# Rows made from the mixer's scaled tiles, the mixer one tile up, and the down groups behind the joint part

## The chip, the cores and the metric

The kernel runs on one core of a Trainium2 chip. A core has TensorE (PE, the matmuls), VectorE (DVE), ScalarE (ACT) and GpSimd (POOL), and DMA queues, of which SyncE (SP) issues most. The metric is the time of one execution on the device in microseconds; lower is better. The time before is a median of three runs.

## The reference

The model has two layers over 1024 tokens of 1024 channels. Each layer is a token mixer and a SwiGLU FFN of 2816 columns, each behind an RMSNorm that is scaled and shifted by a conditioning vector. Layer 0 mixes by a causal convolution, layer 1 by trailing means:

```python
for i in range(DEPTH):
    sh_m, sc_m, g_m, sh_f, sc_f, g_f = split(silu(c) @ ada_w[i] + ada_b[i])
    h = modulate(rms_norm(x, norm_mix_g[i]), sh_m, sc_m)
    y = conformer_conv(h, ...) if i % 2 == 0 else multiscale_pool(h, ...)
    x = x + (1.0 + g_m) * y
    h = modulate(rms_norm(x, norm_ffn_g[i]), sh_f, sc_f)
    y = (silu(h @ w_gate) * (h @ w_up)) @ w_down
    x = x + (1.0 + g_f) * y
return rms_norm(x, final_g)
```

`multiscale_pool` takes, in four groups of channels, the mean of the last 2, 4, 8 or 16 tokens less the token, then a 256 by 256 matrix per group and a scale. All data is float32.

## The kernel before

Activations lie as 8 tiles (`KT`) of 128 channels by 512 tokens for each of two chunks of tokens, A (index 0) and B (index 1). A float32 product is made of three products of rounded halves: each tile is split into a high part (`hhi`, `ghi`, made by ACT) and a low part (`hlo`, `glo`, made by DVE or POOL as the tile less its high part), and weights likewise. So one 128-channel step costs three matmuls; the gate and up products of one ff-tile (128 of the 2816 columns) are 48 matmuls, and the down products of two ff-tiles for one chunk (`ffn_p2`) are 48 too.

The change lies in layer 1, around what is called the joint part. First, ff-tiles 0 to 7 of chunk A run plainly: the list `us` holds units in the order gate/up of f (`ffn_p1`), down products of the two tiles before (`ffn_p2`), gate/up of f + 1, and so on. While TensorE does that, chunk B's pool mixer runs on the other engines: its root (sum of squares, `var` and `rstd` as small matmuls, then the scaled tiles `t<-x,gains,ny`), its windows (`win`), the mixed tiles split into `mxhi` and `mxlo`, then on TensorE the `y` matmuls (48), whose results are added to `x` (`pool_out`). Then B's second norm is made (`norm`, giving `hhi` and `hlo` of B).

Then comes the joint part for ff-tiles 8 to 21 of both chunks. There the products of A and B with the two halves of the channels are formed by a scheme with fewer products, which takes combined operands: `joint_rows` makes the rows t1, t2, t3, t4 (each four tiles, split into high and low) from the tiles of A and B. It rebuilds each whole tile by adding high and low part. t1, t4 and the first half of B's normed tiles (`front`) are put into DRAM (`keep`) and streamed back later, since there is no room. `joint_unit` runs one unit: `block(..., "w11")`, `block(..., "w12")`, then the block on t2, on t1, on t3 and the rest, for gate, then for up. The first unit also runs the down products of A's tiles 6 and 7 behind its first blocks.

Behind the joint part stand the last two groups of its down products, which `alone` emits one after the other (48 + 48 matmuls); outputs go to the two spare PSUM banks there. Then `ffn_mixed` does ff-tiles 0 to 7 of chunk B: `before` holds gate/up of f = 0 and of f = 1, `pairs` the rest.

The order on TensorE is written by hand: `add`, `unit` and `need` append units to a list that is emitted in that order. The other engines' tasks are generators (`put`), of which the tile framework's priorities set the order: an urgent or eager task (`put_eager`) goes first, others have lower priority. `PSUM` has 8 banks, which `output(name, spread)` hands out. Tags of pools and their buffer counts say how many tiles of a kind there are (`"acc"`, `"win"`, `"ada"`, `"raw"`).

Of the kernel before, what the change touches and what calls it, by code (L numbers as in the profile page):

```python
# [16 lines left out]
P = 128  # L17
D = 1024
# [45 lines left out]
T2_AT, T3_AT = ((0, 1), (0, 1), (1, 0), (1, 0)), ((0, 1), (1, 0), (0, 1), (0, 1))  # L64
# [58 lines left out]
def trunk(ctx, tc, xT, c, vec, ada, adan, w1, w2, wgu, wdn, wpl, wph, out):  # L123
# [455 lines left out]
    def norm(ch, l, ffn, key, keep=False, squares=None, ks=range(KT), **kw):  # L579
# [7 lines left out]
        for k in ks:  # L587
# [398 lines left out]
    def ffn_p1(ch, l, f, pick, soon=False):  # L986
        def emit(take):
# [189 lines left out]
    class Downs:  # L1177
# [25 lines left out]
        def slot(self):  # L1203
# [198 lines left out]

    def joint_rows():

        ha, hb = st["h", 0], st["h", 1]
        half = KT // 2
        for name in ("t1", "t4", "front"):
            st["kept", name] = [[kept.tile([P, 512], F32, name=nm(name)) for _ in range(2)] for _ in range(half)]
        st["t1"], st["t2"], st["t3"] = [], [], []

# [9 lines left out]
        def whole(h, t):  # L1420
            V_.tensor_tensor(t, f32(h[0]), f32(h[1]), op=ADD)
            return t
        for k in range(half):
            keep("front", k, hb[k])
            a, c, d = whole(ha[k], window(512, "ha")), whole(hb[k], window(512, "hb")), whole(hb[k + half], window(512, "hb"))
            yield
            V_.tensor_tensor(a, a, c, op=SUB)
            V_.tensor_tensor(c, d, c, op=SUB)
            V_.scalar_tensor_tensor(d, a, -1.0, d, op0=MUL, op1=SUB)
            st["t2"].append(split(d, [wslot(B, n, F32R, at * ALIGN, 512) for n, at in zip(("t2hi", "t2lo"), T2_AT[k])]))  # L1430
            yield
            b = whole(ha[k + half], temp(512))
            V_.scalar_tensor_tensor(b, d, -1.0, b, op0=MUL, op1=SUB)
# [3 lines left out]
            st["t3"].append(split(c, [wslot(A, n, F32R, at * ALIGN, 512) for n, at in zip(("t3hi", "t3lo"), T3_AT[k])]))  # L1437
# [554 lines left out]
```

## Time and profile before

| | |
|---|---|
| median of 3 runs | 1816.73 us (1815.53 to 1817.51) |
| profiled execution | 1817.02 us |
| its span in the profile | 1815.2 us |
| granted TensorE clock, mean | 0.989 |
| PE busy | 1765.0 us (97%) |
| DVE busy | 1315.9 us (72%) |
| ACT busy | 940.4 us (52%) |
| POOL busy | 513.9 us (28%) |

Busy times are sums over the span; they can overlap. In the rows of the timeline a time stands first, then the length, engine, line, operation, the written tile and what it is made from, and in brackets the idle time of the engine just ahead with the instruction that ended it. L117 and L140 are the lines of helpers that record every vector instruction and every matmul, so rows are told apart by the names of tiles. A row of matmuls xN that starts at one time covers N matmuls in a row.

### The profile page before, as it was taken

The page shows a single profiled execution, that of the slowest core. Times are in us where ns is not written, and L with a number is a line of the kernel's source. Part 1 is how long each engine was busy: PE and PEld are TensorE (multiplying, and loading weights), DVE is VectorE, ACT ScalarE, POOL GpSimd, SP SyncE. Part 2 cuts the span into 40 slices and gives each one's busy share as a digit, 9 for nine tenths or more (in the row PEclk, how much of TensorE's full clock was granted, in tenths as well). Part 3 has the DMA queues.
Part 4 walks back from the last instruction along what each step waited for, and adds up shares of the span by engine and source line. Part 5 has one row for each costly group of instructions (what it writes and reads, how often), then busy time and mean ns, then how long its engine had stood idle before and what let it go on. Part 6 is the DMA issues. An engine that isn't in the chain of part 4 may idle for free. (4 is left out here: it accounts for less than half of the span.)

```text
span 1815.2 us, 24581 instructions
## 1 busy us (share of the span) xinstructions
PE 1765.0 (97%) x8930; PEld 1477.8 (81%) x8930; DVE 1315.9 (72%) x2107; ACT 940.4 (52%) x1439; POOL 513.9 (28%) x550
## 2 busy tenths in 40 slices
PE   9999999999999999999999999997999999998997
PEld 7777777888888887899998888875888888886997
DVE  7689847897764239899887867797666566648685
ACT  4776765777656366555555465444323233333553
POOL 0389723987823111201114414210000000000102
PEclk9999999999999999999999999998999999999999
DMA  9968775989979898877766568756655555584552
GB/s 301 284 179 260 176 165 161 246 206 234 229 196 226 216 226 193 233 201 207 210 171 150 139 155 199 171 151 218 208 186 197 186 197 186 197 268 103 141 150 59
DMA packets 133293, 353.13 MB, mean 195 GB/s; under 512 B 13490, under 2 KB 23858, under 8 KB 133171
## 3 DMA queue, kind: packets, MB, share of 16 engines
q1 hardware_dynamic: 105808, 265.56, 43.0%
q0 software_dynamic: 26208, 84.95, 26.3%
q8 instruction: 70, 1.15, 0.2%
q10 hardware_dynamic: 1154, 1.05, 0.2%
q14 instruction: 53, 0.43, 0.1%
HBM read 341.02 MB, written 10.49 MB: 194 GB/s over the span
## 5 line engine op out<-in xcount | busy, mean ns | idle before, releaser
L117 ACT CAST w<-raw 128x512 fp32r<-128x512 f32 (+1 forms) x338 | 276.5, 822 | 185.5 <-PE dn L140 55.8
L117 DVE SCALAR_TENSOR_TENSOR x<-dn,gains,x 128x512 f32<-128x512 f32 (+1 forms) x360 | 262.0, 735 | 118.3 <-PE dn L140 113.3
L140 PE MATMUL dn<-ghi,w 128*128 128x512 f32 (+1 forms) x992 | 316.6, 386 | 1.4 <-DMA w<-in_wdn_dram 0.8
L140 PE MATMUL gate<-hhi,w 128*128 128x512 f32 (+1 forms) x928 | 284.1, 374 | 0.6 <-ACT hhi L117 0.6
L140 PE MATMUL up<-hhi,w 128*128 128x512 f32 (+1 forms) x928 | 284.5, 374 | 0.0
L117 ACT ACTIVATE w<-raw 128x1024 fp32r<-128x1024 f32 (+1 forms) x182 | 175.5, 964 | 198.0 <-PE up L140 63.5
L117 POOL TENSOR_TENSOR pa<-pa,pr 128x512 f32<-128x512 f32 x176 | 252.8, 1584 | 18.3 <-ACT pr L117 15.5
L452 POOL DMA_DIRECT2D w<-in_wgu_dram x76 | 68.4, 904 | 650.9 <-ACT w L117 641.4
L140 PEld LDWEIGHTS dn<-ghi,w 128*128 128x128 f32 x992 | 185.3, 189 | 37.0 <-DMA w<-in_wdn_dram 1.2
L140 PEld LDWEIGHTS gate<-hhi,w 128*128 128x128 f32 x928 | 171.0, 188 | 32.9 <-ACT hhi L117 0.7
L140 PEld LDWEIGHTS up<-hhi,w 128*128 128x128 f32 x928 | 171.0, 188 | 31.0
L140 PE MATMUL dn<-glo,w 128*128 128x512 f32 (+1 forms) x496 | 191.2, 385 | 3.0 <-POOL glo L117 2.9
L140 PE MATMUL dn<-gpair,w 128*128 128x512 f32 x672 | 173.4, 396 | 8.8 <-DVE x L117 8.7
L140 PE MATMUL gate<-hlo,w 128*128 128x512 f32 (+1 forms) x464 | 173.5, 374 | 0.3 <-DVE hlo L117 0.3
L140 PE MATMUL up<-hlo,w 128*128 128x512 f32 (+1 forms) x464 | 173.3, 374 | 0.0
L117 DVE SCALAR_TENSOR_TENSOR ca<-u,vecs,ca 128x512 f32<-128x512 f32 x244 | 170.6, 747 | 1.0
L140 PEld LDWEIGHTS dn<-gpair,w 128*128 128x128 f32 x672 | 127.8, 191 | 38.8 <-DVE x L117 6.5
L117 DVE TENSOR_TENSOR w<-raw,w 128x512 fp32r<-128x512 f32 (+1 forms) x156 | 121.0, 781 | 35.4 <-ACT w L117 34.2
L117 ACT ACTIVATE pr<-u,vecs 128x512 f32<-128x512 f32 x176 | 120.2, 717 | 29.2 <-POOL pa L117 21.5
L117 DVE TENSOR_TENSOR t<-t,up 128x512 f32<-128x512 f32 (+1 forms) x79 | 51.4, 652 | 108.4 <-PE up L140 107.5
L1168 POOL DMA_DIRECT2D w<-in_wgu_dram x40 | 34.9, 879 | 266.5 <-ACT w L117 81.0
L140 PEld LDWEIGHTS dn<-glo,w 128*128 128x128 f32 x496 | 93.9, 189 | 19.5 <-POOL glo L117 3.9
(254 smaller groups left out, 3327.7 us busy)
## 6 DMA issues: line engine op xcount, KB each, us to landing
raw<-in_wgu_dram SPq DMA_DIRECT2D x148, 512.0 KB, 5.6
t<-t SPq DMA_DIRECT2D x224, 256.0 KB, 5.0
w<-in_wgu_dram POOLq DMA_DIRECT2D x76, 512.0 KB, 8.2
raw<-in_wdn_dram SPq DMA_DIRECT2D x74, 512.0 KB, 5.7
adaw<-in_ada_dram SPq DMA_DIRECT2D x64, 512.0 KB, 4.8
raw<-in_w_dram SPq DMA_DIRECT2D x42, 512.0 KB, 6.6
w<-in_wdn_dram POOLq DMA_DIRECT2D x34, 512.0 KB, 8.0
adaw<-in_adan_dram SPq DMA_DIRECT2D x32, 512.0 KB, 6.6
```

The lines of the kernel that those rows point to most:

```text
L117: self.last = self.order(getattr(self.eng, name)(out, *args, **kw))
L140: last_mm[0] = nc.tensor.matmul(out, lhsT, rhs, start=start, stop=stop, **kw).ins.name
L452: order(nc.gpsimd.dma_start(as_src(lo), src, accum_op=ADD))
L1168: order(nc.gpsimd.dma_start(lo, src, accum_op=ADD))
```

## The change

1. The root of B's pool mixer becomes a task of its own, `stats_whole`, which is urgent; `pool_whole` waits for its result and is eager.
2. `pool_out` and what follows come one unit earlier in `us` (at `len(us) - 5` instead of `len(us) - 4`), so the y matmuls stand ahead of gate/up of ff-tile 5 instead of behind it.
3. `wholes` makes the eight whole tiles of A while the mixer runs. `joint_rows` no longer starts from B's normed halves: it waits for the norm's `rstd` alone, makes each tile of B once as `scaled(k)`, combines from that, and splits only the second half of B's tiles there. `front` is one float32 tile for each k instead of a high and a low one, and is split into `hhi` and `hlo` in the last joint unit. The rows' places (`T2_AT`, `T3_AT`, `TURNED`) change, t4's tiles move from tag `"acc"` (2 buffers) to `"win"` (3). The g tiles of A's ff-tiles 6 and 7 move into `"ada"` tiles (`home`).
4. `alone(second, final)` fetches the final group's down weights with the first group and loads them when 4 outputs are left, and sends its outputs to all 8 banks in turn (`output(n, True)`). Gate/up of B's ff-tile 1 is put between the two groups of 48 down matmuls.

On TensorE, around the y matmuls; names are `up` (up products of an ff-tile), `dn` (down products), `y` (the mixer's products from `mxhi`, `mxlo`). Before:

```order
5329 L140 MATMUL up_10806<-hhi_9856,w_10730 128x512
5330 L140 MATMUL up_10806<-hlo_9857,w_10730 128x512
5331 L140 MATMUL up_10806<-hhi_9856,w_10731 128x512
5332 L140 MATMUL y_10882<-mxhi_10476,w_10801 128x512
5333 L140 MATMUL y_10882<-mxlo_10477,w_10801 128x512
5334 L140 MATMUL y_10882<-mxhi_10476,w_10802 128x512
```

And after:

```order
5281 L141 MATMUL dn_10805<-ghi_10657,w_10675 128x512
5282 L141 MATMUL dn_10805<-glo_10658,w_10675 128x512
5283 L141 MATMUL dn_10805<-ghi_10657,w_10676 128x512
5284 L141 MATMUL y_10827<-mxhi_10399,w_10739 128x512
5285 L141 MATMUL y_10827<-mxlo_10400,w_10739 128x512
5286 L141 MATMUL y_10827<-mxhi_10399,w_10740 128x512
```

Before, the y matmuls follow the up products of ff-tile 5; after, they follow the down products of ff-tiles 2 and 3, and stand 48 rows earlier.

On VectorE, in the middle of the combined rows (`ha`, `hb` are the rebuilt tiles of A and B, `t_` scaled tiles and temporaries, `whole` the tiles of A made ahead, `t1lo` to `t3lo` the low parts of the rows). Before:

```order
1387 L117 TENSOR_TENSOR ha_11491<-hhi_9846,hlo_9847 128x512
1388 L117 TENSOR_TENSOR hb_11493<-hhi_10987,hlo_10988 128x512
1389 L117 TENSOR_TENSOR t2lo_11467<-hb_11461,t2hi_11466 128x512
1390 L117 TENSOR_TENSOR t_2213_11484<-t_11470,t_2212_11483 128x512
1391 L117 TENSOR_TENSOR ha_11491<-ha_11491,hb_11493 128x512
1392 L117 TENSOR_TENSOR hb_11495<-hhi_10995,hlo_10996 128x512
1393 L117 TENSOR_TENSOR hb_11493<-hb_11495,hb_11493 128x512
1394 L117 TENSOR_TENSOR t1lo_11508<-ha_11491,t1hi_11507 128x512
```

And after:

```order
1339 L118 SCALAR_TENSOR_TENSOR t_11109<-whole_10633,t_11109 128x512
1340 L118 TENSOR_TENSOR t_11174<-t_11174,up_11058 128x512
1341 L118 TENSOR_TENSOR hlo_11218<-t_11169,hhi_11217 128x512
1342 L118 SCALAR_TENSOR_TENSOR whole_10653<-t_11109,whole_10653 128x512
1343 L118 SCALAR_TENSOR_TENSOR x_1_80<-dn_11201,gains,x_1_80 128x512
1344 L118 TENSOR_TENSOR t1lo_11289<-whole_10647,t1hi_11288 128x512
1345 L118 TENSOR_TENSOR t2lo_11134<-t_11109,t2hi_11133 128x512
1346 L118 SCALAR_TENSOR_TENSOR x_2_81<-dn_11209,gains,x_2_81 128x512
```

The rebuilding rows (`<-hhi,hlo`) are gone from here, and evictions to x now stand among the combinations.

On TensorE, behind the joint part, at the boundary between the two groups of down matmuls. Before:

```order
7004 L140 MATMUL dn_14946<-gpair_11867,w_14877 128x512 x3
7005 L140 MATMUL dn_14946<-gpair_11868,w_14877 128x512 x3
7006 L140 MATMUL dn_14959<-gpair_11865,w_14956 128x512 x3
7007 L140 MATMUL dn_14959<-gpair_11866,w_14956 128x512 x3
7008 L140 MATMUL dn_14970<-gpair_11867,w_14956 128x512 x3
```

And after:

```order
6972 L141 MATMUL dn_14919<-gpair_11835,w_14855 128x512 x3
6973 L141 MATMUL dn_14919<-gpair_11836,w_14855 128x512 x3
6974 L141 MATMUL gate_14937<-hhi_14586,w_14676 128x512
6975 L141 MATMUL gate_14937<-hlo_14587,w_14676 128x512
6976 L141 MATMUL gate_14937<-hhi_14586,w_14677 128x512
```

The second group no longer follows the first at once; the 48 gate/up matmuls of ff-tile 1 stand between.

The diff, cut to its core:

```diff
 GATE_SLOTS = (6, 9, 12, 14, 17, 19, 22, 24)
-T2_AT, T3_AT = ((0, 1), (0, 1), (1, 0), (1, 0)), ((0, 1), (1, 0), (0, 1), (0, 1))
+T2_AT, T3_AT = ((0, 1), (0, 1), (1, 0), (0, 1)), ((1, 0), (0, 1), (0, 1), (1, 0))
+TURNED = ((27,), (22, 25, 26, 29))
 UP_SLOTS = (3, 6, 9, 11, 14, 17, 20, 23)
...
-    def gated(ch, f, outs, soon=False, held=None):
+    def gated(ch, f, outs, soon=False, held=None, home=None):
 
-        hi, lo = st["g", ch.i, f] = gslots(ch)
+        if home is None:
+            hi, lo = st["g", ch.i, f] = gslots(ch)
+        else:
+            g = raws.tile([P, D], F32R, tag="ada", name=nm("gpair"), bufs=ADA_BUFS)
+            st.setdefault("G", []).append(g)
+            hi, lo = st["g", ch.i, f] = g[:, FRONT], g[:, BACK]
         t = temp(ch.n) if held is None else temp(ch.n, "ny", 2)
...
 
-    def alone(downs):
+    def alone(downs, later=None):
 
         def emit(take):
+            if later is not None:
+                later.fetch()
             while downs.todo:
-                downs.slot()
+                downs.slot(lambda n: output(n, True))
+                if later is not None and len(downs.todo) == 4:
+                    later.load(later.dps[0])
             reserve[0] = 0
...
 
+    def wholes():
+
+        st["whole"] = []
+        for h in st["h", 0]:
+            t = wslot(B, "whole", F32, 0, 512)
+            V_.tensor_tensor(t, f32(h[0]), f32(h[1]), op=ADD)
+            st["whole"].append(t)
+            yield
+
     def joint_rows():
 
-        ha, hb = st["h", 0], st["h", 1]
         half = KT // 2
-        for name in ("t1", "t4", "front"):
+        for name in ("t1", "t4"):
             st["kept", name] = [[kept.tile([P, 512], F32, name=nm(name)) for _ in range(2)] for _ in range(half)]
+        st["kept", "front"] = [kept.tile([P, 512], F32, name=nm("front")) for _ in range(half)]
         st["t1"], st["t2"], st["t3"] = [], [], []
+        hb = st["h", 1] = [None] * KT
+        while ("rstd", 1) not in st:
+            yield "wait"
+        rstd = st.pop(("rstd", 1))
 
...
 
-        def whole(h, t):
-            V_.tensor_tensor(t, f32(h[0]), f32(h[1]), op=ADD)
+        def scaled(k):
+            t = temp(512)
+            V_.scalar_tensor_tensor(t, x[1][k], scale_f[:, KT + k : KT + k + 1], rstd, op0=MUL, op1=MUL)
+            S_.activation(t, t, AF.Identity, bias=shift(1, 3, k))
             return t
         for k in range(half):
-            keep("front", k, hb[k])
-            a, c, d = whole(ha[k], window(512, "ha")), whole(hb[k], window(512, "hb")), whole(hb[k + half], window(512, "hb"))
+            c, d = scaled(k), scaled(k + half)
+            a, b = st["whole"][k], st["whole"][k + half]
+            sync.dma_start(st["kept", "front"][k], c)
             yield
+            hb[k + half] = split(d, (slot(B, "hhi"), slot(B, "hlo")))
             V_.tensor_tensor(a, a, c, op=SUB)
-            V_.tensor_tensor(c, d, c, op=SUB)
-            V_.scalar_tensor_tensor(d, a, -1.0, d, op0=MUL, op1=SUB)
-            st["t2"].append(split(d, [wslot(B, n, F32R, at * ALIGN, 512) for n, at in zip(("t2hi", "t2lo"), T2_AT[k])]))
+            e = window(512, "hb")
+            V_.tensor_tensor(e, d, c, op=SUB)
             yield
-            b = whole(ha[k + half], temp(512))
+            V_.scalar_tensor_tensor(d, a, -1.0, d, op0=MUL, op1=SUB)
+            st["t2"].append(split(d, [wslot(B if k else A, n, F32R, at * ALIGN, 512) for n, at in zip(("t2hi", "t2lo"), T2_AT[k])]))
             V_.scalar_tensor_tensor(b, d, -1.0, b, op0=MUL, op1=SUB)
+            yield
             st["t1"].append(split(a, [slot(B, n) for n in ("t1hi", "t1lo")]))
...
             yield
-            st["t3"].append(split(c, [wslot(A, n, F32R, at * ALIGN, 512) for n, at in zip(("t3hi", "t3lo"), T3_AT[k])]))
-            keep("t4", k, split(b, [tmp.tile([P, TMPW], F32R, tag="acc", name=nm("t4"), bufs=2) for _ in range(2)]))
+            st["t3"].append(split(e, [wslot(A if k < half - 1 else B, n, F32R, at * ALIGN, 512) for n, at in zip(("t3hi", "t3lo"), T3_AT[k])]))
+            keep("t4", k, split(b, [tmp.tile([P, PHALO + TMPW], F32R, tag="win", name=nm("t4"), bufs=3)[:, :512] for _ in range(2)]))
             yield
...
             V_.tensor_tensor(ra, ra, left, op=ADD)
+            if last:
+                front = []
+                for src in st["kept", "front"]:
+                    t = slot(A, "front", F32)
+                    sync.dma_start(t, src)
+                    hi, lo = slot(A, "hhi"), slot(A, "hlo")
+                    S_.copy(hi, t)
+                    V_.tensor_tensor(lo, t, f32(hi), op=SUB)
+                    front.append((hi, lo))
             if first:
...
             if last:
-                st["h", 1] = [tuple(t) for t in streamed("front", A)] + hb[half:]
+                st["h", 1] = front + hb[half:]
             else:
...
                 V_.scalar_tensor_tensor(qb, qb, -1.0, sg[2], op0=MUL, op1=MUL)
-                if "G" not in st:
-                    st["G"] = [raws.tile([P, D], F32R, tag="ada", name=nm("gpair"), bufs=ADA_BUFS) for _ in range(2)]
+                if len(st["G"]) == 2:
                     st["G"] += [raws.tile([P, D], F32R, tag="raw", name=nm("gpair")), wide("gpair", F32R)]
...
                                  i == 0, i + 1 == len(mates)))
-        return us, [alone(d) for d in (mine[-2][0], mine[-1][0])]
+        (second,), (final,) = mine[-2:]
+        return us, [alone(second, final), alone(final)]
 
...
 
-    def pool_whole(ch):
+    def stats_whole(ch):
         acc = yield from sum_sq(x[ch.i], ch.n)
-        st["spread", ch.i] = mean_rsqrt(acc, ch.n, True, "col2")
+        st["rstd", ch.i] = yield from mean_rsqrt(acc, ch.n, True, "col2")
+
+    def given(key):
+        return st.pop(key)
+        yield
+
+    def pool_whole(ch):
+        while ("rstd", ch.i) not in st:
+            yield "wait"
+        st["spread", ch.i] = given(("rstd", ch.i))
         yield from pool(ch)
+        T["wholes"] = Task(wholes(), False, 0)
+        T["wholes"].eager = True
+
+    def mixed_norm(squares):
+        st["rstd", 1] = yield from mean_rsqrt(squares.acc, 512, True)
 
...
     for f in range(0, WHOLE, 2):
-        us += [ffn_p1(A, 1, f, True), joint_pend, ffn_p1(A, 1, f + 1, True)]
+        home = True if f + 2 == WHOLE else None
+        us += [ffn_p1(A, 1, f, True, home=home), joint_pend, ffn_p1(A, 1, f + 1, True, home=home)]
         joint_pend = ffn_p2(A, 1, [f, f + 1], True)
...
         if i == 1:
-            put(("pool", 1), lambda: pool_whole(B), at=0, delay=DELAY_AMONG)
-        if i == len(us) - 4:
+            put(("stats", 1), lambda: stats_whole(B), True, delay=DELAY_AMONG)
+            put_eager(("pool", 1), lambda: pool_whole(B))
+        if i == len(us) - 5:
             need(("pool", 1))
...
                 pool_out(B, 1, q, squares)
-            put(("nf", 1), lambda: norm(B, 1, True, ("hn", 1), True, squares, [k + q for k in range(KT // 2) for q in (0, KT // 2)]),
-                True, delay=DELAY_AMONG)
+            put(("nf", 1), lambda: mixed_norm(squares), True, delay=DELAY_AMONG)
+            put_eager("rows", joint_rows)
     need(("nf", 1))
-    unit(lambda take: st.__setitem__(("h", 1), st["hn", 1]))
-    put_eager("rows", joint_rows)
     joint, last = ffn_joint(1, WHOLE)
     add(joint)
-    unit(lambda take: setattr(B, "made", B.made + KT // 2))
     before, pairs, rest = ffn_mixed(B, 1, 2, WHOLE, True, ("final_a", lambda: final(A)))
...
     put_eager(("T", 1), lambda: combined(B, (A, A, B, B)))
-    add(last)
-    add(before[1:])
+    add(last[:1] + before[1:] + last[1:])
     paired(B, pairs)
```

More of the change, by code (lines that the diff above doesn't have):

```diff
@@ L264, in gslots @@
         turned = ch.i == 0 and ch.made >= NF and (ch.made - NF) % 4 == 0
-        odd = (ch.made // (KT // 2) + ch.i + turned) % 2
+        odd = (ch.made // (KT // 2) + ch.i + turned + (ch.made in TURNED[ch.i])) % 2
         ch.made += 1
@@ L577, in modulated, with norm @@
             lows.append(V_.last.ins.name)
-    def norm(ch, l, ffn, key, keep=False, squares=None, ks=range(KT), **kw):
+    def norm(ch, l, ffn, key, keep=False, squares=None, **kw):
         h = [(slot(ch, "hhi"), slot(ch, "hlo")) for _ in range(KT)]
@@ L586, in norm @@
         lows = []
-        for k in ks:
+        for k in range(KT):
             modulated(ch, l, ffn, h, rstd, k, lows if kw else None)
@@ L983, in update, with ffn_p1 @@
         V_.scalar_tensor_tensor(xs, b, gate[:, l * KT + d : l * KT + d + 1], xs, op0=MUL, op1=ADD)
-    def ffn_p1(ch, l, f, pick, soon=False):
+    def ffn_p1(ch, l, f, pick, soon=False, home=None):
         def emit(take):
@@ L995, in emit @@
                         pace()
-            gated(ch, f, outs, soon)
+            gated(ch, f, outs, soon, home=home)
         return emit, (wgu[l, f, 0], wgu[l, f, 1])
-    def gated(ch, f, outs, soon=False, held=None):
-        hi, lo = st["g", ch.i, f] = gslots(ch)
+    def gated(ch, f, outs, soon=False, held=None, home=None):
[5 more added lines that the diff above has]
+            hi, lo = st["g", ch.i, f] = g[:, FRONT], g[:, BACK]
         t = temp(ch.n) if held is None else temp(ch.n, "ny", 2)
@@ L1201, in load, with slot @@
             self.tiles[dp] = wt
-        def slot(self):
+        def slot(self, out=None):
             d = self.todo.pop(0)
@@ L1896, in trunk @@
     pooled(rest[:-1], A, OUT_AT)
+    def stats_whole(ch):
+        acc = yield from sum_sq(x[ch.i], ch.n)
+        st["rstd", ch.i] = yield from mean_rsqrt(acc, ch.n, True, "col2")
+    def given(key):
+        return st.pop(key)
+        yield
     def pool_whole(ch):
-        acc = yield from sum_sq(x[ch.i], ch.n)
-        st["spread", ch.i] = mean_rsqrt(acc, ch.n, True, "col2")
+        while ("rstd", ch.i) not in st:
+            yield "wait"
+        st["spread", ch.i] = given(("rstd", ch.i))
         yield from pool(ch)
+        T["wholes"] = Task(wholes(), False, 0)
+        T["wholes"].eager = True
+    def mixed_norm(squares):
+        st["rstd", 1] = yield from mean_rsqrt(squares.acc, 512, True)
     us, joint_pend = [], rest[-1]
     for f in range(0, WHOLE, 2):
-        us += [ffn_p1(A, 1, f, True), joint_pend, ffn_p1(A, 1, f + 1, True)]
+        home = True if f + 2 == WHOLE else None
+        us += [ffn_p1(A, 1, f, True, home=home), joint_pend, ffn_p1(A, 1, f + 1, True, home=home)]
         joint_pend = ffn_p2(A, 1, [f, f + 1], True)
```

2 lines of the change are left out of this document (1 added, 1 removed).

## The prediction

> **What bounds the kernel now.** I read the stretches of 40 us first, then the waits of TensorE, then its rows and VectorE's in the two stretches where it is short. Columns of the first view: busy time and instructions of PE, PEld, DVE, ACT and POOL, the granted clock, the DMA share, GB/s.
>
> ```profile
> 1160.00:1200.00 40.00, 40.00 (x186) 33.40 (x185) 32.16 (x59) 22.47 (x34) 3.50 (x4) 1.00 0.74 186
> 1200.00:1240.00 40.00, 25.77 (x95) 18.87 (x93) 39.35 (x65) 13.04 (x23) 4.52 (x1) 0.83 0.41 145
> 1240.00:1280.00 40.00, 37.54 (x154) 30.19 (x155) 27.75 (x45) 18.49 (x32) 0.00 (x0) 0.92 0.76 260
> 1280.00:1320.00 40.00, 40.00 (x179) 33.10 (x178) 22.45 (x33) 10.96 (x20) 0.00 (x0) 1.00 0.50 174
> 1640.00:1680.00 40.00, 31.29 (x118) 23.63 (x117) 33.90 (x61) 13.37 (x23) 1.75 (x2) 0.91 0.36 90
> ```
>
> TensorE is full at clock 1.00 in the first and fourth row and short in the other three. In 1200 to 1240 VectorE is the full one (39.35 of 40). The waits name what was late, as total, times and longest:
>
> ```profile
> PE gate L140 <- ACT t2hi L117: 10.0, 3, 3.6
> PE dn L140 <- DVE x L117: 8.7, 5, 3.3
> PE gate L140 <- DVE t2lo L117: 3.8, 3, 1.9
> PE dn L140 <- POOL glo L117: 2.9, 1, 2.9
> ```
>
> So there are two places: one ahead of the joint part, where the combined rows t2 and a low piece of ff-tile 6 are late (10.0 + 3.8 + 2.9 = 16.7 us), and one behind it, where down matmuls wait for evictions to x (8.7 us). The rows of the first place:
>
> ```profile
> 1182.45 2.74 DVE L117 SCALAR_TENSOR_TENSOR t<-x,gains,ny 128x512 f32<-128x512 f32 x4
> 1204.95 1.28 DVE L117 TENSOR_TENSOR t<-t,up 128x512 f32<-128x512 f32 x2
> 1207.07 4.52 POOL L117 TENSOR_TENSOR glo<-t,ghi 128x512 fp32r<-128x512 f32 x1 [24.50 <-ACT ghi L117]
> 1208.40 0.39 PE L140 MATMUL dn<-ghi,w 128*128 128x512 f32 x1
> 1211.64 0.50 PE L140 MATMUL dn<-glo,w 128*128 128x512 f32 x1 [2.86 <-POOL glo L117]
> 1212.71 1.05 PE L140 MATMUL dn<-ghi,w 128*128 128x512 f32 x2
> 1216.09 0.40 PE L140 MATMUL dn<-glo,w 128*128 128x512 f32 x1
> 1224.04 0.39 PE L140 MATMUL gate<-t2hi,w 128*128 128x512 f32 x1
> 1228.53 0.51 PE L140 MATMUL gate<-t2hi,w 128*128 128x512 f32 x1 [3.64 <-ACT t2hi L117]
> 1242.44 0.69 DVE L117 TENSOR_TENSOR t2lo<-hb,t2hi 128x512 fp32r<-128x512 f32 x1
> 1256.32 0.39 PE L140 MATMUL up<-hhi,w 128*128 128x512 f32 x1
> ```
>
> PE reaches the t2 block at 1224.04, VectorE finishes the last t2lo only at 1243.1, and the next full-speed block (up) starts at 1256.32. And of the second place, with the clock there in its pitch:
>
> ```profile
> 1646.37 2.88 PE L140 MATMUL dn<-gpair,w 128*128 128x512 f32 x12
> 1652.55 4.61 PE L140 MATMUL dn<-gpair,w 128*128 128x512 f32 x12 [3.30 <-DVE x L117]
> 1659.52 4.56 PE L140 MATMUL dn<-gpair,w 128*128 128x512 f32 x12 [2.35 <-DVE x L117]
> ...
> 1692.64 1.60 PE L140 MATMUL gate<-front,w 128*128 128x256 f32 x12
> ```
>
> Twelve matmuls take 2.88 us undisturbed: (2.88 - 0.39) / 11 = 0.2265 us each, so a block of 48 is 10.9 us. Right after a wait the same twelve take 4.61 us: a wait costs itself and up to 1.73 us of slow clock. The granted clock shows it too (0.91).
>
> **Behind the joint part (`alone`, order of `last`).** Between 1646.37 and 1692.64 there are 96 down matmuls and the 48 of B's ff-tile 1: 144 x 0.2265 = 32.6 us of work in 46.3 us. The 13.7 us of difference are 8.7 of waits and about 5 of slow clock. Before, only two spare banks take the down outputs; each output is six matmuls (1.36 us), and its bank is free only after an eviction. After the change the outputs rotate over all eight banks, and the 48 matmuls of ff-tile 1 stand between the two groups of 48, so VectorE has 10.9 us of PE work that needs no eviction in which to catch up. VectorE's evictions, 16 at the 0.66 us pitch that the first row of the next part shows, are 10.6 us of a span of 32.6, so it is no bound by sum. What remains is order: other rows (weight sums of the next unit) stand in front of evictions on VectorE, and one of them waits for a raw weight load, which I put 1 to 3 us ahead of need. Bounds: all 13.7 back, or a third of it lost as one new wait of about 3 us with its clock (3 + 1.7 = 4.7, leaving 9.0). I take **12.5**. The earlier fetch of the second group's down weights is a move of DMA issues to an earlier place on SP's queue; the window there has a DMA share of 0.36, which hides them; without that cover one 512 KB load would delay the first pair by a few us, which the lower bound holds.
>
> **The combined rows.** What VectorE spends per row, in its busiest stretch (busy us, mean ns):
>
> ```profile
> L117 DVE SCALAR_TENSOR_TENSOR x<-dn,gains,x 128x512 f32<-128x512 f32 x16 | 11.7, 747 | 0.0
> L117 DVE SCALAR_TENSOR_TENSOR hlo<-t,mod,hhi 128x512 fp32r<-128x512 f32 x8 | 5.6, 749 | 0.0
> L117 DVE TENSOR_TENSOR hb<-hhi,hlo 128x512 f32<-128x512 f32 x8 | 5.5, 686 | 0.0
> L117 DVE TENSOR_TENSOR t<-hhi,hlo 128x512 f32<-128x512 f32 x4 | 2.8, 688 | 0.6 <-POOL glo L117 0.6
> L117 DVE TENSOR_TENSOR ha<-hhi,hlo 128x512 f32<-128x512 f32 x3 | 2.1, 685 | 0.0
> L117 POOL TENSOR_TENSOR glo<-t,ghi x14: 1283/1311/4522, 366.8 to 1207.1; 128x512 fp32r<-128x512 f32 x14
> ```
>
> Four rows of one group take 2.74 us in the timeline above, so the pitch is 0.66 us for an STT row (three operands) and 0.60 for a two-operand row. Before, 64 rows make the combinations; after, 44 do: gone are the 8 `hb<-hhi,hlo`, 8 rebuilt sums of A (moved ahead into the mixing) and 4 of the 8 `hlo`. That is 20 x 0.60 to 0.66 = 12 to 13 us less on the engine that is full. The stores of `front` fall from 8 to 4; four splits return later in the last joint unit, where VectorE is at 22 of 40 (the fourth stretch), so I charge nothing: PE there doesn't wait for it.
>
> The second gain is the start. The change puts the mixer's 48 y matmuls one tile earlier, ahead of ff-tile 5 instead of behind it, so what follows them (root, first scaled row) comes 10.9 us earlier less 0.4 for smaller shifts in its place among the matmuls. The rows start at about **1172.2** instead of 1182.45. The last t2lo is the 67th row from there: 67 x 0.62 = 41.5, plus 1 to 2 us in which VectorE waits for ACT, gives 1215, before PE wants it. So **the t2 waits vanish** (13.8 us and their slow clock).
>
> What is late next: ff-tile 7's product `t<-t,up`, which stood at 1204.95 and now is the 60th row from the start: 22 STT x 0.66 + 37 others x 0.60 = 36.7, plus 1.5 of ACT waits, gives 1210.4. ACT's high piece ends 1.3 us on (1211.7); then its low piece, now always on POOL, takes 1.31 us (median above) to 4.52 (the row at 1207.07): 1213.0 to 1216.2. TensorE gets to it three matmuls after 1208.40, at 1209.1 (the blocks ahead of it are the same 96 matmuls in another order). So PE idles 3.9 to 7.1 us; I take 5.4, plus 1.7 of slow clock. The t2 block then starts at 1208.4 + 10.9 + 5.4 + 1.7 = 1226.4, its 60 matmuls take 13.6, and up starts at 1240.0 against 1256.32: **16.3 us** gained. With no wait at all it would be 1232.9, so 23.4 gained; with the late ends on all of these (7.1, two slow-clock spells, 2 us of waits left in t2) 13.
>
> [...]
>
> **The mixer one tile up.** Its cover is the slack of the mixing:
>
> ```profile
> 1093.22 0.95 PE L140 MATMUL var<-ones,acc 128*128 128x1 f32 x8
> 1102.29 1.05 PE L140 MATMUL rstd<-ident,col 128*128 128x128 f32 x8
> 1105.43 3.52 DVE L117 SCALAR_TENSOR_TENSOR t<-x,gains,ny 128x512 f32<-128x512 f32 x4
> 1149.78 0.68 DVE L117 TENSOR_TENSOR mxlo<-win,mxhi 128x512 fp32r<-128x512 f32 x1
> 1157.61 0.39 PE L140 MATMUL y<-mxhi,w 128*128 128x512 f32 x1
> ```
>
> Before, the last low piece ends at 1150.5, 7.1 us ahead of y; y is now wanted at 1157.61 - 10.9 = 1146.7. The urgent root takes rstd 36 matmuls up, 8.2 us, so the scaled rows start at 1097.2. Before, mixing is 56 VectorE rows from there to the last piece in 45.1 us (0.80 each, with the waits for POOL among them); after, 55, since the eight sums of A come in as evictions move out. So it ends at about 1097.2 + 44.3 = 1141.5, some 5 us early. Tighter is the down block ahead of y (1135.8): it needs ff-tile 3's low piece at 1136.5, whose product is now the 45th of those rows, at 1097.2 + 36 = 1133.2, with ACT and POOL behind it (0.6 + 1.3 and gaps) 1136. A stall is between 0 and 5 (3.3 and its clock); I take **1**, since the slack is about zero. Without the earlier root it would be some 8 us.
>
> **The sum.** 12.5 + 16.3 - 1 = 27.8. The profiled execution took 1817.0 (0.3 over the median of 1816.73): 1817.0 - 27.8 = 1789.2, so **1789**.
>
> **The rivals.** *Low pieces in time* (POOL quick, root early enough): 23.4 + 13.7 = 37.1, so 1780; for it speaks the median of POOL, against it that f7's product is 60 rows deep. *Late at several points*: the mixing's down block stalls 5, f7 idles 7.1 and t2 still waits 2 to 3, gain 13 - 4 + 9 = 18, so 1796 to 1802; for it speaks VectorE's 39.35 of 40. *Only the part behind the joint part works* (rows not earlier, since something between root and rows still sits in TensorE's order): 1804. *No gain at all*, the idle time only moving to the start of the next unit, 1817: against it speaks that the stretch from 1280 is full with VectorE at 22.45 of 40. *Slower*, by one mechanism: SP's queue runs in order, and a store of a t4 tile now stands behind a weight load that waits for its slot; t4 has three buffers, so ACT's next t4hi, and with it every later row on ACT, waits for the store.
>
> ```profile
> SPq L1115 <- DVE acc L117: 71.5, 18, 10.4
> ```
>
> Such a load waits 71.5 / 18 = 4.0 us on average, 10.4 at the longest. Four stores at 4.0 are 16 us, and the t2 rows have 11 us of room (1215 against 1226.4), so a mean case costs a few us; the whole is slower than before only from (11 + 27.8) / 4 = 9.7 us for each store, the longest wait four times over: 1817 to 1825.
>
> **How the numbers follow.** My forecast, 1785 to 1794: 0.5. Low pieces in time, 1780 to 1785: 0.15. Late at several points, 1794 to 1802: 0.22. One place alone, 1802 to 1813: 0.06. No gain: 0.03. Slower by the stores: 0.04. The range 1780 to 1801 leaves out the last three, and little else. A difference under 0.2% (3.6 us) is not told from none by a measurement of this kernel: faster 0.93, same 0.03, slower 0.04.
>
> **What would show it.** In the changed kernel's profile: no wait of `gate` for t2hi or t2lo; one wait of `dn` for a gpair from POOL, 4 to 7 us, near 1209; up of the first joint unit near 1240; y near 1147 with no idle time before it; behind the joint part 48 + 48 + 48 matmuls in 33 to 37 us without waits for x. Wrong would be: waits of `dn` for x behind the joint part, a long wait ahead of y, SP waits that ACT's t4 rows inherit, or a new wait in the first joint unit for streamed tiles.

## The result and the profile after

The changed kernel takes 1790.64 us (median of 4 runs, 1788.28 to 1793.23) against 1817.12 for the kernel before: a ratio of 0.9852, 95% interval 0.983 to 0.9873. The forecast was 1789 in a range of 1780 to 1801. The profiled execution took 1788.28 us, the shortest of the four, with a span of 1786.5. The kernels below ran in later rounds beside the kernel before, whose median was 1816.7 to 1818.0 us in them (one run of 2630.84 us in the slow state, at a clock of 0.625, left out), so about 1 us of a difference between medians of two rounds may come from the rounds.

The stretches of 40 us that answer to those of before (busy time and instructions of PE, PEld, DVE, ACT and POOL, granted clock, DMA share, GB/s):

```profile
1160.00:1200.00 40.00, 35.57 (x153) 28.86 (x152) 30.20 (x55) 23.21 (x36) 6.52 (x6) 0.91 0.84 224
1200.00:1240.00 40.00, 39.53 (x175) 32.42 (x174) 34.19 (x54) 18.16 (x32) 4.65 (x1) 1.00 0.49 170
1240.00:1280.00 40.00, 40.00 (x178) 32.91 (x177) 23.16 (x35) 14.32 (x25) 0.00 (x0) 1.00 0.69 239
1600.00:1640.00 40.00, 38.33 (x168) 31.12 (x167) 26.70 (x48) 18.29 (x29) 3.48 (x4) 1.00 0.69 187
1640.00:1680.00 40.00, 40.00 (x237) 35.61 (x236) 35.49 (x60) 20.20 (x40) 4.36 (x5) 1.00 0.59 150
```

The three short stretches of before are now full or nearly so (39.53, 40.00 and 40.00 us). Two others have become short: 1160 to 1200, which was full, and a little of 1600 to 1640. TensorE's waits (total, times, longest) name them:

```profile
PE dn L141 <- ACT ghi L118: 3.4, 1, 3.4
PE dn L141 <- ACT w L118: 1.7, 1, 1.7
...
PE dn L141 <- POOL glo L118: 1.1, 1, 1.1
...
PE dn L141 <- POOL gpair L118: 0.5, 1, 0.5
```

No wait for t2 and none for x behind the joint part is left; in their place stands one for `ghi`, of ff-tile 5. The place in the timelines of the changed kernel, TensorE first, then the other engines' rows that it hangs on:

```profile
1134.41 0.39 PE L141 MATMUL dn<-ghi,w 128*128 128x512 f32 x1
1145.38 0.39 PE L141 MATMUL y<-mxhi,w 128*128 128x512 f32 x1
1168.04 1.05 PE L141 MATMUL rstd<-ident,col 128*128 128x128 f32 x8
1179.85 0.39 PE L141 MATMUL dn<-ghi,w 128*128 128x512 f32 x1
1184.05 0.59 PE L141 MATMUL dn<-ghi,w 128*128 128x512 f32 x1 [3.36 <-ACT ghi L118]
1185.71 0.80 PE L141 MATMUL dn<-glo,w 128*128 128x512 f32 x1 [1.07 <-POOL glo L118]
1198.35 0.39 PE L141 MATMUL gate<-hhi,w 128*128 128x512 f32 x1
1216.20 10.27 PE L141 MATMUL dn<-gpair,w 128*128 128x512 f32 x44 [0.47 <-POOL gpair L118]
1226.31 0.39 PE L141 MATMUL gate<-t2hi,w 128*128 128x512 f32 x1
1239.91 0.39 PE L141 MATMUL up<-hhi,w 128*128 128x512 f32 x1
```

```profile
1170.53 2.08 DVE L118 SCALAR_TENSOR_TENSOR t<-x,gains,ny 128x512 f32<-128x512 f32 x3 [5.46 <-ACT ny L118]
1172.52 0.68 DVE L118 TENSOR_TENSOR t<-t,up 128x512 f32<-128x512 f32 x1
1183.38 0.61 ACT L118 CAST ghi<-t 128x512 fp32r<-128x512 f32 x1
1191.45 1.45 POOL L118 TENSOR_TENSOR gpair<-t,gpair 128x512 fp32r<-128x512 f32 x1 [5.80 <-ACT gpair L118]
1210.09 0.68 DVE L118 TENSOR_TENSOR t<-t,up 128x512 f32<-128x512 f32 x1
1211.50 4.65 POOL L118 TENSOR_TENSOR gpair<-t,gpair 128x512 fp32r<-128x512 f32 x1 [18.60 <-DMA raw<-in_wgu_dram]
1214.31 0.68 DVE L118 TENSOR_TENSOR t2lo<-t,t2hi 128x512 fp32r<-128x512 f32 x1
```

The product of ff-tile 5 is there at 1173.2, but ScalarE casts its high part only at 1183.38, behind eleven other instructions: seven for the combined rows, whose task is eager, and four for weights. The block of 48 at 1179.85 ends at 1198.35: 18.5 us for 10.9. The t2 block at 1226.31 then runs 13.6 us with no wait. Behind the joint part all is as the bare count of matmuls says:

```profile
1631.26 9.00 PE L141 MATMUL dn<-gpair,w 128*128 128x512 f32 x39
...
1642.14 0.39 PE L141 MATMUL gate<-hhi,w 128*128 128x512 f32 x1
...
1653.02 11.04 PE L141 MATMUL dn<-gpair,w 128*128 128x512 f32 x48
1663.90 0.28 PE L141 MATMUL gate<-hhi,w 128*128 128x256 f32 x1
```

A mark that both kernels share is the start of the down block of A's ff-tiles 2 and 3. It is at 1134.41 here, and in the kernel before at

```profile
1135.85 0.39 PE L140 MATMUL dn<-ghi,w 128*128 128x512 f32 x1
```

so the times of the two traces are compared as distances from it. From it to the first up unit of the joint part: 120.47 before (to 1256.32), 105.50 now: **15.0 us**. From there to the pairs, whose first row is the gate row of 128x256: 436.32 before, 423.99 now: **12.3 us**, made of 13.6 behind the joint part (46.27 less 32.64) and 1.3 lost on the way, most of it near 1603: the last up half of the joint part takes 32.16 us, 30.59 before. From the pairs to the end both take 122.6. The mark itself lies 1.4 earlier; it moves from run to run (1133.10 in the kernel before with only the last part changed), so that is not put down to the change. With it, this is the 28.7 between the two profiled executions; the medians differ by 26.5.

### The profile page after: what moved, and what is told of

Its sections match the earlier page's. It is cut to its first block, busy times and chain, and to the rows that moved or that the text cites. A ratio compares the mean times of both kernels' runs of the same rounds, so it can differ in the third digit from the quotient of the medians.

```text
span 1786.5 us, 24555 instructions
## 1 busy us (share of the span) xinstructions
PE 1756.9 (98%) x8930; PEld 1475.3 (83%) x8930; DVE 1309.4 (73%) x2095; ACT 943.2 (53%) x1447; POOL 518.1 (29%) x554
## 4 chain that ended last, share of the span: by engine, by line
PE 87%; DVE 5%; issue 3%; DMA 2%; ACT 2%; POOL 1%; SPq 0%; DVEq 0%; POOLq 0%; ACTq 0%
PE dn L141 24%; PE gate L141 23%; PE up L141 23%; PE y L141 5%; PE a L141 3%; PE g L141 2%; PE first L141 2%; DVE x L118 1%; ACT w L118 1%; DVE t L118 1%; PE ada L141 1%; PE var L141 1%; ACT t L118 1%; PE idle L141 1%; DMA adaw<-in_adan_dram 1%
## 5 line engine op out<-in xcount | busy, mean ns | idle before, releaser
L141 PE MATMUL dn<-ghi,w 128*128 128x512 f32 (+1 forms) x960 | 307.1, 387 | 3.9 <-ACT ghi L118 3.4
L141 PE MATMUL up<-hhi,w 128*128 128x512 f32 (+1 forms) x968 | 294.5, 372 | 0.0
L141 PE MATMUL gate<-hhi,w 128*128 128x512 f32 (+1 forms) x968 | 293.7, 372 | 0.6 <-ACT hhi L118 0.6
L141 PEld LDWEIGHTS gate<-hhi,w 128*128 128x128 f32 x968 | 177.8, 188 | 33.7 <-ACT hhi L118 0.8
L141 PEld LDWEIGHTS up<-hhi,w 128*128 128x128 f32 x968 | 177.9, 188 | 31.7
L141 PE MATMUL dn<-glo,w 128*128 128x512 f32 (+1 forms) x480 | 185.5, 387 | 1.2 <-POOL glo L118 1.1
L141 PE MATMUL dn<-gpair,w 128*128 128x512 f32 x720 | 180.0, 390 | 2.1 <-ACT w L118 1.7
L141 PE MATMUL gate<-hlo,w 128*128 128x512 f32 (+1 forms) x484 | 180.0, 372 | 0.3 <-DVE hlo L118 0.3
L141 PE MATMUL up<-hlo,w 128*128 128x512 f32 (+1 forms) x484 | 179.8, 372 | 0.0
L141 PEld LDWEIGHTS dn<-gpair,w 128*128 128x128 f32 x720 | 134.9, 188 | 31.3 <-ACT w L118 2.1
```

The lines of the kernel that those rows point to most:

```text
L141: last_mm[0] = nc.tensor.matmul(out, lhsT, rhs, start=start, stop=stop, **kw).ins.name
```

## The experiments

**The part behind the joint part, alone, undone, and split in two.** These four ran against the same runs of the kernel before. In the first the last part is undone:

```diff
-        return us, [alone(second, final), alone(final)]
+        return us, [alone(d) for d in (mine[-2][0], mine[-1][0])]
-    add(last[:1] + before[1:] + last[1:])
+    add(last)
+    add(before[1:])
-                downs.slot(lambda n: output(n, True))
+                downs.slot()
```

> The changed kernel with its last part undone: behind the joint part stand two groups of 48 down matmuls one after the other on two spare banks, then gate/up of ff-tile 1. If the two places add up (theory), this stretch takes 46 us again instead of 32.6, and the time is 1790.6 + 13.6 = 1804 (1802 to 1806), that is 13 less than the kernel before. Rival: the two places share something (VectorE's backlog carried through the joint part), then the old tail on the new front costs less than 9.

Measured: 1801.75 us, ratio 0.992 (0.9903 to 0.9936), just under the range: it costs 11.1 us against the changed kernel, not 13.6. TensorE waits 6.9 us for x again, and up to pairs takes 435.76 us, the 436.32 of before. The fourth is the kernel before with this part alone:

> The kernel before with only the change behind the joint part (banks, order, earlier fetch). Theory: independent of what stands ahead of the joint part, it gains 13.6 us: 1817.1 - 13.6 = 1803.5 (1802 to 1806). Rival: part of the gain needs the changed layout of tiles ahead of it, then under 9.

Measured: 1802.46 us, ratio 0.9919 (0.9904 to 0.9934), 14.2 us less than before. The two halves give 14.2 and (1816.69 - 1801.75) 14.9, in sum 29.1, somewhat over the 26.5 of both together; so they add up, but for 2 to 3 us. Next, the order without the banks:

```diff
-                downs.slot(lambda n: output(n, True))
+                downs.slot()
```

> The changed kernel with the two spare banks for the down outputs behind the joint part, but ff-tile 1 kept between the two groups. Theory: the banks are what the waits for x are about (an output of 1.36 us against an eviction that stands behind weight sums on VectorE), so most of the waits come back: 5 to 9 us slower than the changed kernel, 1796 to 1800. Rival: the 48 matmuls between give VectorE room enough; then at most 3 us slower.

and the banks without the order:

```diff
-    add(last[:1] + before[1:] + last[1:])
+    add(last)
+    add(before[1:])
```

> The changed kernel with all eight banks for the down outputs, but both groups of 48 in a row and ff-tile 1 behind them as before. Theory: eight banks let VectorE lag by eight outputs, which is 10.9 us of TensorE's time, so the waits for x nearly vanish: 0 to 3 us slower than the changed kernel, 1790.6 to 1794. Rival: the order is what counts (VectorE has 33.9 us of work in 40 there, and 16 evictions at the end of it): 5 to 9 us slower.

Measured: 1800.45 us (ratio 0.9908, 0.9893 to 0.9923) with the order alone, 9.8 us slower than the changed kernel and so a little worse than forecast, and 1791.7 (0.986, 0.9845 to 0.9875) with the banks alone, as forecast. In the first, the waits of TensorE for x, and in the second its down block, as one row of the timeline:

```profile
PE dn L141 <- DVE x L118: 6.3, 4, 3.6
```

```profile
1632.83 21.92 PE L141 MATMUL dn<-gpair,w 128*128 128x512 f32 x96
```

With eight banks 96 matmuls run in a row with no wait; the banks are nearly all of it. With two banks the waits fall mostly on the first group of 48 (7.1 of the 8.7 us in the kernel before, 5.8 of the 6.9 in the one with the last part undone, all 6.3 with the order alone), so gate/up of ff-tile 1 behind that group come too late to help: the order is worth about 1 us, within the scatter. The earlier fetch was not taken away by itself; it stands in both kernels, and with the order it is worth 1.3 us (1801.75 to 1800.45). How an eviction comes to be late shows in VectorE's rows of the kernel before. The first six down matmuls, from 1646.37, are done by 1647.9, but rows of weights and of the next unit stand on VectorE ahead of their eviction:

```profile
1651.15 0.69 DVE L117 TENSOR_TENSOR hf<-front,front 128x512 f32<-128x512 f32 x1
1651.75 0.75 DVE L117 SCALAR_TENSOR_TENSOR x<-dn,gains,x 128x512 f32<-128x512 f32 x1
```

It ends at 1652.50, and the down matmuls that wait for it go on at 1652.55.

**The mixer's place and its root.** First the root as an ordinary task:

```diff
-            put(("stats", 1), lambda: stats_whole(B), True, delay=DELAY_AMONG)
+            put(("stats", 1), lambda: stats_whole(B), at=0, delay=DELAY_AMONG)
```

> The changed kernel with the mixer's root as an ordinary task, not an urgent one. Theory, as predicted: the mixing starts up to 8.2 us later, and the down and y matmuls ahead wait 3 to 8 us: 1794 to 1799. Rival: the mixing has slack (measured: no wait ahead of y at 1145.4), then under 2 us slower.

Measured: 1799.02 us, ratio 0.9892 (0.9874 to 0.991), 8.4 us slower than the changed kernel, at the upper end of what was forecast. Its waits around y:

```profile
PE var L141 <- DVE acc L118: 2.5, 1, 2.5
PE y L141 <- DVE x L118: 1.0, 2, 0.6
PE y L141 <- DVE mxlo L118: 0.8, 1, 0.8
```

The y products wait for evictions and for a mixed tile, and the norm's `var` then for its sum. The down block ahead of y, which the prediction called the tighter spot, waits 0.22 us only. From the mark to up it takes 114.63 us, 9.1 more than in the changed kernel: 4.5 of these waits, 0.9 of longer waits for ff-tiles 5 and 7 (5.8 us against 4.9), the rest in matmuls that took longer behind waits, as the eight of `var` did (1.87 us, 0.95 in the changed kernel). Without the early root the move of y gives back all that it gains, as the next kernel shows, which has the root and not the move and takes as long. It puts the y matmuls, the norm and the rows one unit later, where they stood:

```diff
-        if i == len(us) - 5:
+        if i == len(us) - 4:
```

> The changed kernel with the y matmuls, the norm and the rows one unit later, where they stood before; the shorter rows stay. Theory: the rows start 10.5 us later (1181); TensorE doesn't stall for ff-tile 5 (its high part is ahead), but the rows' last t2lo is the 81st row from the start, 1181 + 52 = 1233, against a t2 block reached at about 1220, so waits for t2 of 5 to 10 us return with their clock: 1793 to 1800. Rival: the shorter rows alone do it and the unit's place is worth nothing: within 2 us of the changed kernel.

Measured: 1799.1 us, ratio 0.99 (0.9885 to 0.9916), 8.5 us slower than the changed kernel. The t2 waits come back as forecast, 5.6 us in all, and with them a wait of 5.12 us for ff-tile 7's low piece, which was not forecast here:

```profile
1217.67 11.74 PE L141 MATMUL dn<-gpair,w 128*128 128x512 f32 x44 [5.12 <-POOL gpair L118]
1231.46 0.50 PE L141 MATMUL gate<-t2lo,w 128*128 128x512 f32 x1 [0.43 <-DVE t2lo L118]
1236.99 0.80 PE L141 MATMUL gate<-t2hi,w 128*128 128x512 f32 x1 [4.79 <-ACT t2hi L118]
```

So of the 15.0 us ahead of the joint part the shorter rows give about 7 (mark to up is 113.32 here, 120.47 before) and the place one unit earlier about 8.

**Why ff-tile 5's stall cost nothing.** The rows start one unit later in the program, behind gate/up of ff-tile 5, so that ScalarE's cast of its high part comes ahead of their work:

```diff
-            put_eager("rows", joint_rows)
+        if i == len(us) - 4:
+            put_eager("rows", joint_rows)
```

> The changed kernel with the combined rows started one unit later in the program, behind gate/up of ff-tile 5, so that ScalarE makes ff-tile 5's high part ahead of the rows' work instead of behind eleven of its instructions. The 3.36 + 1.07 us of waits of the down matmuls near 1184 and their 3.2 us of slow clock go. Theory: VectorE's backlog of rows is the bound, so ff-tile 7's product comes no earlier than 1208 (56 rows from 1170.5), its low piece on GpSimd at 1211 to 1214, TensorE wants it at 1207.7, and a wait of 3 to 6 us with its clock takes the place of the old one: 0 to 4 us faster than the changed kernel, 1787 to 1790.6. Rival: the stall of ff-tile 5 was pure loss, and all 7.6 us come back: 1783.

Measured: 1790.44 us, ratio 0.9852 (0.9837 to 0.9868), the changed kernel's own. The stall near 1184 is gone, and the one that the prediction had named stands in its place:

```profile
1209.11 6.41 POOL L118 TENSOR_TENSOR gpair<-t,gpair 128x512 fp32r<-128x512 f32 x1 [21.73 <-ACT gpair L118]
1215.58 12.21 PE L141 MATMUL dn<-gpair,w 128*128 128x512 f32 x44 [5.49 <-POOL gpair L118]
1241.30 0.39 PE L141 MATMUL up<-hhi,w 128*128 128x512 f32 x1
```

TensorE gets to ff-tile 7 earlier and waits 5.49 us for its low piece; from the mark (1135.51) to up it is 105.79 us, against 105.50. The theory of VectorE's backlog holds against the rival of a pure loss. Now GpSimd's piece is taken away, too, by putting both low pieces on VectorE:

```diff
-        (V_ if soon else either(ch.n)).tensor_tensor(lo, t, hi.bitcast(F32), op=SUB)
+        (V_ if soon or home is not None else either(ch.n)).tensor_tensor(lo, t, hi.bitcast(F32), op=SUB)
```

> The kernel with rows behind ff-tile 5, and the low pieces of ff-tiles 6 and 7 on VectorE instead of GpSimd. Theory: VectorE's queue is full there, so the low piece (the 66th row from the start, 1213) is no earlier than GpSimd's, and the time is that of the kernel with rows behind ff-tile 5 within 2 us. Rival: GpSimd's slow 4.65 us piece is the bound, then 2 to 4 us faster than that kernel.

Measured: 1789.87 us, ratio 0.9846 (0.9831 to 0.9862): not to be told from the last. In place, the wait falls from 5.49 to 0.68 + 3.07 us and mark to up from 105.79 to 104.16. To see whether VectorE's count of rows is what remains, twelve of them are left out: the low parts of t1, t3 and t4, for which the high part stands:

```diff
-            V_.tensor_tensor(tiles[1], q, f32(tiles[0]), op=SUB)
-            return tiles
+            if low:
+                V_.tensor_tensor(tiles[1], q, f32(tiles[0]), op=SUB)
+            return tiles if low else [tiles[0], tiles[0]]
```

> The kernel with rows behind ff-tile 5 and the low pieces of ff-tiles 6 and 7 on VectorE, with the low parts of t1, t3 and t4 left out (their high part stands for both, so twelve VectorE rows are not computed). Theory: with 12 rows less in VectorE's backlog the low piece of ff-tile 7 (56th row) is there at about 1207, TensorE doesn't wait near 1209, and the time is 5 us less than with them: 1785. Rival: the wait hangs on ScalarE or on the order, not on VectorE's count of rows: then unchanged.

Measured: 1784.52 us, ratio 0.9821 (0.9807 to 0.9834), 5.4 less than the median with them. The down block of ff-tiles 6 and 7 runs with no wait:

```profile
1208.03 11.04 PE L141 MATMUL dn<-gpair,w 128*128 128x512 f32 x48
1218.91 0.40 PE L141 MATMUL gate<-t2hi,w 128*128 128x512 f32 x1
```

That shows the bound at this place: VectorE's rows ahead of ff-tile 7. Two kernels take rows off VectorE by giving them to GpSimd. In the first the four t1lo go there:

```diff
-            st["t1"].append(split(a, [slot(B, n) for n in ("t1hi", "t1lo")]))
+            st["t1"].append(split(a, [slot(B, n) for n in ("t1hi", "t1lo")], G_))
```

> The kernel with rows behind ff-tile 5 and the low pieces of ff-tiles 6 and 7 on VectorE, and now the four t1lo on GpSimd, which stands idle there. Theory: VectorE's count of rows ahead of ff-tile 7 is the bound. Its product moves from the 59th to the 50th row and its low piece from the 66th to the 58th, 1207.6 instead of 1213, so the waits of 0.7 + 3.1 us and their 1.7 of slow clock shrink to under 1: 4 to 5 us faster than the kernel with both low pieces on VectorE, 1785. Rival: GpSimd's pieces (6.4 us each beside a full VectorE) hold up tiles that VectorE needs, and nothing is gained or it is slower.

Measured: 1789.45 us, ratio 0.9853 (0.9839 to 0.9866); the forecast of 1785 missed. In place the first half came true and the second was not foreseen:

```profile
1210.41 10.28 PE L141 MATMUL dn<-gpair,w 128*128 128x512 f32 x44 [1.64 <-DVE gpair L118]
1235.66 0.73 PE L141 MATMUL gate<-t,w 128*128 128x512 f32 x2 [1.75 <-DMA t<-t]
```

The wait is 1.64 us instead of 3.75, but the last t4lo moved from the 77th to the 82nd row, and the tiles that are streamed back arrive 1.75 us late. The second puts the four t3lo on GpSimd as well (the same edit at `st["t3"]`):

> As the kernel with the four t1lo on GpSimd, and the four t3lo there too, so VectorE has eight rows less. Theory: ff-tile 7's low piece is the 55th row (1206) and the last t4lo the 77th instead of the 82nd, so both the wait near 1209 (1.6 us with t1lo alone) and the one for the streamed t4 tiles (1.75 us) go: 3 us faster than with t1lo alone, 1785 to 1787, near the 1784.5 of the kernel without these low parts. Rival: GpSimd takes 5 us or more for each of its eight pieces beside a full VectorE, and the t1 or t3 block waits for it: no gain or a loss.

Measured: 1787.75 us, ratio 0.9839 (0.9825 to 0.9852), 1.7 us faster than with t1lo alone where 3 was forecast. Mark to up is 100.21 us (97.35 without the twelve rows, 101.97 with t1lo moved alone); one wait of 2.03 us for ff-tile 7 stays, the streamed tiles are in time. Its median is 2.9 us under that of the changed kernel; the intervals of the two ratios overlap (0.9825 to 0.9852 against 0.983 to 0.9873), so a gain over it isn't shown. Part of what is gained ahead is lost further on: from up to the pairs it takes 426.98 us, the changed kernel 423.99. Of these 3.0 us, 2.1 lie in the last up half of the joint part (34.30 us against 32.16), at the wait of the next paragraph. The kernels with rows behind ff-tile 5 and with both low pieces on VectorE (with or without the low parts) lose 1.5 to 1.7 there, too.

**The wait that is new near 1603.** ScalarE splits front's tiles in the last joint unit and stands waiting for their loads, with a weight cast behind it:

```profile
1603.34 0.62 ACT L118 CAST hhi<-front 128x512 fp32r<-128x512 f32 x1 [0.94 <-DMA front<-front]
1604.34 0.62 ACT L118 CAST w<-raw 128x512 fp32r<-128x512 f32 x1
```

```profile
1605.02 1.92 PE L141 MATMUL dn<-gpair,w 128*128 128x512 f32 x6 [1.67 <-ACT w L118]
```

The splits are moved to the end of the unit, behind its products:

```diff
-                    S_.copy(hi, t)
-                    V_.tensor_tensor(lo, t, f32(hi), op=SUB)
...
+                for t, hi, lo in front:
+                    S_.copy(hi, t)
+                    tc.add_manual_dep(S_.last.ins, last_mm[0], edge, reason="behind the products")
+                    V_.tensor_tensor(lo, t, f32(hi), op=SUB)
```

> The kernel with rows behind ff-tile 5 and the low pieces of ff-tiles 6 and 7 on VectorE, with the four splits of front in the last joint unit put behind the weight casts of that unit on ScalarE. Theory: the one wait that the changed kernel has new behind the joint part's start (1.5 to 1.8 us of dn for w near 1603, with about 0.4 of slow clock) comes from ScalarE waiting for front's loads; it goes, 2 us faster: 1788. Rival: the cast is late for its own load; unchanged.

Measured: 1792.55 us (1788.32 to 1795.39), ratio 0.9863 (0.9846 to 0.988): no gain, against 1788 forecast. The wait for w is gone, and TensorE waits for the split's own product a little later:

```profile
1625.33 0.50 PE L141 MATMUL gate<-hlo,w 128*128 128x512 f32 x1 [1.27 <-DVE hlo L118]
```

The last up half and the gate products behind it take 30.67 + 9.13 = 39.80 us, against 33.70 + 5.44 = 39.14 without the move. So both spots are narrow there: too early the split holds up a weight cast, too late the next gate product. Between the two nothing was tried.

## Why the prediction was right, and where not

- **Behind the joint part**: 12.5 forecast, 13.6 measured, the full difference. The mechanism (an output's bank free only after an eviction that stands behind other rows) holds, shown by the kernels with the banks and with the order alone. That the 48 matmuls of ff-tile 1 give VectorE room was wrong as a cause: most waits fall ahead of them.
- **The combined rows**: the t2 waits vanished as forecast; the rows began at 1170.53 (1172.2 forecast), ff-tile 7's product stood at 1210.09 (1210.4) and the last t2lo at 1214.31 (1215). They are the 60th and the 67th row from there, as counted.
- **What is late next**: this step failed in its place. It held that TensorE gets to ff-tile 7 at 1209.1, since the blocks ahead of it are the same matmuls. It got there at 1215.7, because ScalarE cast ff-tile 5's high part only at 1183.38, and ScalarE's queue was not followed past the moved tile. What sets the end is as forecast, ff-tile 7's low piece: with the first stall removed, the second shows up at once, and up starts 105.8 us behind the mark instead of 105.5. That the unforeseen stall (4.4 of waits and 3.2 of slow clock, granted 0.83 from 1179 to 1199) was about as long as the forecast one (5.4 + 1.7) was luck: TensorE reached ff-tile 7's low piece 0.47 us before it was ready, and a longer stall would have cost its excess in full. The term was 16.3; measured from the mark it is 15.0.
- **GpSimd's low piece**: forecast between 1.31 and 4.52 us, measured 4.65, and 6.41 in the kernel with rows behind ff-tile 5. The piece of 4.65 us ended 1.24 us after VectorE had come to a row with an input in PSUM (`t<-t,gate`, last section). ff-tile 6's piece, with VectorE as full, took 1.45; there VectorE was at such a row (`x<-dn`, 1191.66), and its next row, with no input in PSUM (`t1lo`, 1192.32), took 1.13 us instead of 0.68.
- **The mixer one tile up**: 1 us of stall forecast, none measured: the block at 1134.41 takes 10.97 and y follows at once. The cover was thin, as forecast: ff-tile 3's low piece ended at 1133.87, 1.4 us ahead of its matmul at 1135.31, and the last mixed piece at 1140.96, 4.4 us ahead of y. Without the early root it costs 8.4 us (some 8 forecast), though at y and `var` and not in the down block.
- **Front's splits** were charged with nothing, since VectorE had room. The term was missed on ScalarE, not for want of room (18.29 of 40 us busy there) but by its order: the split waits for its load and a weight cast stands behind it. That is 1.67 us of wait, and the six matmuls behind it took 1.92 us instead of 1.52; the up half of the last joint unit takes 32.16 us against 30.59 before.
- **The slower rival**, stores of t4 behind weight loads on SP's queue, did not show: ScalarE's waits from 1165 to 1230 name no store of t4, and the last t2lo came earlier than forecast. The one store that held up a row of VectorE or ScalarE there was of front, not of t4: VectorE's scaled row at 1178.28 waited 0.87 us for it.

## What to carry to other kernels

When a unit is moved ahead in one engine's hand-written order, follow what its helpers' eager work does to the casts of the unit that now stands behind it, on every engine: the new stall came from ScalarE's queue, not from the engine that was full. A stall that disappears without gain was covered by a later one; a kernel that leaves out rows of the suspected engine shows which of the two is the bound. Where outputs wait for evictions, give them all the banks first and reorder afterwards.

## What the runs showed of the hardware

What a wait cost beyond itself went by its length at one place and not at another. The same 44 down matmuls took 10.27 or 10.28 us behind waits of 0.47, 1.38, 1.64 and 2.03 us, and 11.90, 11.89, 11.74 and 12.21 us behind 2.82, 3.07, 5.12 and 5.49 us; so the four longer waits cost 1.5 to 1.9 us on top, the shorter ones nothing. Near 1605 it was otherwise: in the kernel with both low pieces on VectorE, six matmuls took a full third longer than in the changed kernel, behind a wait that is shorter (2.65 us behind 1.55, against 1.92 behind 1.67 and 1.52 undisturbed), and the six behind them took 2.43 us against 1.53. In the kernel with rows behind ff-tile 5 the same twelve took 2.68 and 2.40 us, behind a wait of 1.71; the granted clock was 0.88 from 1605 to 1610 and 0.78 from 1610 to 1615 there, and 1.00 from 1605 to 1610.5 in the changed kernel. In the kernel with both low pieces on VectorE the two places read:

```profile
1213.39 11.89 PE L141 MATMUL dn<-gpair,w 128*128 128x512 f32 x44 [3.07 <-DVE gpair L118]
...
1605.14 2.65 PE L141 MATMUL dn<-gpair,w 128*128 128x512 f32 x6 [1.55 <-ACT w L118]
```

So for nearly equal short waits the price changes from kernel to kernel, and gaps of 1.55, 2.82 and 3.07 us were paid for here. What sets the price is not shown.

GpSimd's low piece of 128x512 took between 1.3 us (`t1lo` at 1190.17 in the kernel with t1lo on GpSimd) and 6.4 us (rows behind ff-tile 5), beside a VectorE that is full in both cases but for the last 1.1 us of the second. VectorE's rows beside it show where a long piece ended. The one of 4.65 us in the changed kernel ends at 1216.15. The quickest low piece in the kernel before took 1.28 us, and about as long ahead of that end, 1.24 us, VectorE comes to the first row since the piece began that has an input in PSUM (`gate`); the row behind it is stretched from 0.68 to 1.19 us:

```profile
1214.91 0.67 DVE L118 TENSOR_TENSOR t<-t,gate 128x512 f32<-128x512 f32 x1
1215.51 1.19 DVE L118 TENSOR_TENSOR acc<-raw 128x512 f32<-128x512 f32 x1
```

Four more pieces of over 2 us stand beside VectorE's rows. Three of them end 1.23 to 1.25 us after VectorE starts the first such row: the one of 4.52 us in the kernel before (`t<-t,gate`, 1210.36), the one of 2.14 us from 1185.24 with rows behind ff-tile 5 (`x<-dn`, 1186.13), and the one of 5.62 us below. The fourth, of 6.41 us with rows behind ff-tile 5, ends 1.1 us after the last of VectorE's rows ahead of an idle stretch of 2.44 us. So these long pieces ended behind such a row or an idle VectorE; that they wait for it is the author's reading of the traces, and no kernel was made to try it. In the kernel with t1lo on GpSimd the last of the four t1lo took

```profile
1207.70 5.62 POOL L118 TENSOR_TENSOR t1lo<-whole,t1hi 128x512 fp32r<-128x512 f32 x1 [16.23 <-ACT t1hi L118]
```

and VectorE's row with `gate` starts at 1212.09, 1.23 us ahead of its end. A short piece also ran beside rows without an input in PSUM, and there a row of VectorE was the longer one: beside `glo` of 1.58 us, from 1184.08 in the changed kernel, the row at 1184.42 took 1.78 us instead of 0.68. What decides between the two cases is open.
